# A hybrid streaming layer on one core: down projection in groups of 8, 8 and 6 blocks, later differences, row stores from GpSimd, splits queued behind their loads

## The chip, the cores and the metric

The kernel runs on one core of a Trainium2 chip. Its engines work side by side, each through a queue of its own in a fixed order: TensorE (PE in the profile, with PEld for its weight loads), VectorE (DVE), ScalarE (ACT), GpSimd (POOL) and SyncE (SP), which here only issues DMAs. The metric is the device time of one execution in microseconds (us).

## The reference

One inference step of a one-layer encoder, for 1024 rows of a new stream and 64 of a running one: a mixer (a state-space scan beside differential attention) and then a convolutional feed-forward. The change lies in the feed-forward alone:

```python
h = _rmsnorm(x, p['norm_ffn_w']) @ p['w_up']            # (1088, 1024) @ (1024, 5632)
ha, hb = jnp.split(h, 2, axis=-1)
hc, ffn_new = _causal_dwconv(ffn_past, ha, p['ffn_conv_w'], p['ffn_conv_b'])
x = x + (jax.nn.silu(hc) * hb) @ p['w_down']            # (1088, 2816) @ (2816, 1024)
```

All is float32. The kernel makes a float32 product out of three faster ones: each operand is split into a high part, which is a rounded copy, and a low part, which is the rest; the terms high x high, high x low and low x high are added up in PSUM.

## The kernel before, in words

**Strassen's scheme.** Both products of the feed-forward are done by a scheme with 7 products of half-size blocks in place of 8 (variables p = 0 to 6). The left operand is the weight, the right one the activation. Each product needs a left part and a right part, which are blocks or sums and differences of blocks. The right parts are cut in two halves of columns (s = 0, 1) of 272 tokens each.

**The way up** runs over 22 pairs f (`FT`): a pair gives 128 rows of `ha` and 128 of `hb`. A pair has 14 steps (p, s) of 12 matmuls. GpSimd multiplies the gated rows (`put`, L1242 to L1245), and the row goes to the scratch tensor `h_sc` in DRAM through SP, in two halves (L1245).

**The way down** multiplies 22 blocks of 128 rows of `h_sc`. They are taken in groups; `DOWN` lists their sizes, 6, 8 and 8. A group of size 2n has four down pairs i, so i = 0 to 3 belong to the first group, 4 to 7 to the second, 8 to 11 to the last; each of the 14 steps of a pair has 3n matmuls of 272 columns (L1390). Every result of 128 x 544 is added to the output in DRAM by a DMA that accumulates, issued by GpSimd (`send`, L1372 to L1376; the last pair of all stores its final quarter through SP, L1414). Results leave PSUM by ScalarE (p = 0 and 2) and VectorE (the other p), L1393 to L1412: these are the evacuations. Pairs 0, 3, 4, 7, 8 and 11 take all steps of s = 0 ahead of s = 1, in the order `ORD`; the others take s = 0 and 1 in turn.

**Right parts of the way down.** Three of seven are rows of `h_sc` as they are (p = 0, 2, 6); four are differences, made ahead by `differences_of` (L1304 to L1315): for a couple of rows, one of each half of a group, it loads both rows from `h_sc` into tiles `ht`, does four subtractions on VectorE and stores both to the scratch tensor `t_sc`. There are as many couples as half blocks, 11 in all. In the way up, pair f makes the couple whose later row was finished two pairs before (L1436 to L1439). The last two couples of the last group come too late for that; they are made after down pairs 1 and 2 (L1462, L1463).

`right_part` (L1320 to L1331) loads one part (n blocks x 272 columns, 408 KB or 544 KB) through SP and splits it: ScalarE makes the high part (L1042), VectorE the low one (L1043). The 14 parts of a group stay for all its four pairs. They are loaded in the last pair before the group, i.e. f = 21, i = 3 and i = 7. Each takes the place of the part that the step just done has freed (`right_parts`, L1333 to L1347). Some begin sooner: as many as there are spare places. One place is an extra one, made of two rows of the tag `fb`, in which such a part is called `ph`. Since the step order of a group isn't the order in which parts are loaded, a group can have two parts in `ph` rows.

**Buffers.** `ROWS` gives each tag a number of rows. The tag `fb` has four, for `cc` (one for each pair of the way up), `ht` (two for each couple) and `ph` (two for each part). A new tile of a tag waits until a row is free.

**Left parts** (`left_parts`, L1123 to L1165): two loads of a weight block (`w_f`, two buffers, L1129), four sums on GpSimd (L1133, L1134, L1158, L1162) and seven splits. They are made for the next pair, one or so for each step with s = 1 (`more_left`).

**What sets the order.** The instructions are written down in the order of the code, and a planner sorts them into the engines' queues by its own model of the times: where several are ready, the earlier one in the code goes first, and a later one that is ready may pass an earlier one that isn't. On the chip each queue is worked off strictly in that order, so an instruction that waits holds all that stand behind it in its queue. `tc.issue_after(x)` lets the instructions of a block stand behind x in x's queue; it is no wait for x to end.

Of the kernel before, what the change touches and what calls it, by code (L numbers as in the profile page):

```python
# [12 lines left out]
ALU = mybir.AluOpType  # L13
# [4 lines left out]
P = 128  # L18
# [11 lines left out]
FT = DFF // P  # L30
NORM = (128, 256, 192, 192, 192, 128)
LN_EXP = "natural_log_exp_and_others"
DOWN = (6, 8, 8)
ORD = (0, 1, 5, 2, 3, 4, 6)
QW = T // 4
ROWS = dict(fa=4, fb=4, fu=4, fs=2, fp=3, fh=2)
PARTS = ("b11", "t2", "b21", "t3", "t1", "t4", "b22")
# [43 lines left out]
def hybrid_layer(ctx: ExitStack, tc: tile.TileContext, xT, xt, prm, cst, rope, wvd, win, wbs, wba, wout, wup, wdn,  # L81
# [4 lines left out]
    load = nc.sync.dma_start  # L86
# [954 lines left out]
    def split(hi, lo, src):  # L1041
        S.copy(hi, src)  # L1042
        V.tensor_tensor(out=lo, in0=src, in1=hi, op=ALU.subtract)  # L1043
# [166 lines left out]
    def pair(f):  # L1210

        pre = [row("fp", "pre") for _ in range(2)]
        hb = [row("fh", "hb") for _ in range(2)]
        u1, u2 = (couple(row("fu", n)) for n in ("u1", "u2"))
        both = row("fb", "cc")
        G.memset(pre[0][:, 0:2], 0.0)
        G.tensor_copy(pre[1][:, 482:484], par[:, O_FS + 2 * f : O_FS + 2 * f + 2])
        banks = {}

        def pile(key, p, s, start):  # L1220
            if start:
                banks[key, s] = acc(QW)
            ps, w, b = banks[key, s], left[f][p], B[PARTS[p], s]
            for k in range(4):
                c = slice(P * k, P * (k + 1))
                for i, (x, y) in enumerate(((0, 0), (0, 1), (1, 0))):
                    PE.matmul(ps, w[x][:, c], b[y][:, k], start=start and k == i == 0, stop=k == 3 and i == 2,  # L1227
                              skip_group_check=not start)
            return ps

        def gate(h):

            n = 544 + 2 * h
            cc = both[:, 548 * h : 548 * h + 548]
            cw = lambda i: col(O_FW + 3 * f + i)
            act(cc[:, :n], pre[h][:, :n], AF.Identity, bias=col(O_FB + f), scale=cw(0))
            for i in range(1, 3):
                V.scalar_tensor_tensor(cc[:, :n], pre[h][:, i : i + n], cw(i), cc[:, :n], ALU.mult, ALU.add)  # L1238
            act(cc[:, :n], cc[:, :n], AF.Silu)
            return cc  # L1240

        def put(h, cc):  # L1242
            for o, d, n in ((0, 0, 544),) if h == 0 else ((0, 0, 480), (480, 482, 64)):
                G.tensor_tensor(out=hb[h][:, o : o + n], in0=hb[h][:, o : o + n], in1=cc[:, d : d + n], op=ALU.mult)  # L1244
            load(out=h_sc[P * f : P * (f + 1), 544 * h : 544 * (h + 1)], in_=hb[h][:, :544])  # L1245

        at = yield
        for _ in range(14):
            p, s = at
            qs = slice(QW * s, QW * (s + 1))  # L1250
            if p == 0:
                S.copy(u1[:, s], pile("a", p, s, True))
            elif p == 1:
                V.tensor_tensor(out=u2[:, s], in0=pile("b", p, s, True), in1=u1[:, s], op=ALU.add)
            elif p == 2:
                S.copy(pre[0][:, 2 + QW * s : 2 + QW * (s + 1)], pile("a", p, s, False))
                if s == 1:
                    G.tensor_copy(pre[1][:, 0:2], pre[0][:, 544:546])
                    cc0 = gate(0)
            elif p == 3:  # L1260
                V.tensor_tensor(out=u1[:, s], in0=pile("b", p, s, False), in1=u1[:, s], op=ALU.add)
            elif p == 4:
                V.tensor_tensor(out=hb[1][:, qs], in0=pile("c", p, s, True), in1=u1[:, s], op=ALU.add)  # L1263
            elif p == 5:
                V.tensor_tensor(out=hb[0][:, qs], in0=pile("d", p, s, True), in1=u1[:, s], op=ALU.add)
# [17 lines left out]
    def more_left(f):  # L1283
        x = next(coming, None)
        if x is not None:
            left.setdefault(f, {})[x[0]] = x[1]
# [28 lines left out]
            load(out=t_sc[P * (i + n * u) : P * (i + n * u + 1), :], in_=t[u])  # L1315

    SOURCE = {0: (h_sc, 0, 0), 1: (t_sc, 1, 1), 2: (h_sc, 1, 0), 3: (t_sc, 0, 1), 4: (t_sc, 0, 0), 5: (t_sc, 1, 0), 6: (h_sc, 1, 1)}
    parts, held, spare = {}, {}, []

    def right_part(g, p, s, at):  # L1320

        n = DOWN[g] // 2
        d, half, c = SOURCE[p]
        r = P * (first[g] + n * half)
        hi, lo = [unit(*x) if at is not None else couple(row("fb", "ph", R32), 4) for x in at or (0, 1)]
        hi, lo = hi[:, :n], lo[:, :n]
        raw = lo.bitcast(F32)
        load(out=raw, in_=d[r : r + P * n, QW * (2 * c + s) : QW * (2 * c + s + 1)].rearrange("(k p) t -> p k t", p=P))
        split(hi, lo, raw)
        parts[g, s, p] = hi, lo  # L1330
        held[s, p] = at  # L1331

    def right_parts(g, order):  # L1333

# [21 lines left out]
    def down_pair(i):  # L1356
# [22 lines left out]
        while at is not None:  # L1379
            p, s = at  # L1380
            qs = slice(QW * s, QW * (s + 1))
            key = ("a", "b", "a", "b", "c", "d", "e" if apart else "c")[p], s
            start = key not in banks
            if start:
                banks[key] = acc(QW)
            ps, w, b = banks[key], left[FT + i][p], parts[g, s, p]
            for k in range(n):
                c = slice(P * k, P * (k + 1))
                for j, (y, z) in enumerate(((0, 0), (0, 1), (1, 0))):
                    PE.matmul(ps, w[y][:, c], b[z][:, k], start=start and k == j == 0, stop=k == n - 1 and j == 2,  # L1390
                              skip_group_check=not start)
            if p == 0:
                S.copy(u1[:, qs], ps)  # L1393
            elif p == 1:
                V.tensor_tensor(out=u2[:, qs], in0=ps, in1=u1[:, qs], op=ALU.add)
            elif p == 2:
                S.copy(quadrant(2, "fp")[:, qs], ps)
                send(2, s, 0, 0)
            elif p == 3:
                V.tensor_tensor(out=u1[:, qs], in0=ps, in1=u1[:, qs], op=ALU.add)  # L1400
            elif p == 4:
                V.tensor_tensor(out=quadrant(4, "fh")[:, qs], in0=ps, in1=u1[:, qs], op=ALU.add)
                if apart:
                    V.tensor_tensor(out=u2[:, qs], in0=ps, in1=u2[:, qs], op=ALU.add)
                if end:
                    V.tensor_tensor(out=u2[:, qs], in0=base[:, qs], in1=u2[:, qs], op=ALU.add)
                send(4, s, 1, 1)
            if p == 5 and not apart or p == 3 and apart:
                V.tensor_tensor(out=quadrant(5, "fp")[:, qs], in0=banks["d", s], in1=u1[:, qs], op=ALU.add)
                send(5, s, 1, 0)  # L1410
            if p == 6:
                V.tensor_tensor(out=quadrant(6, "fh")[:, qs], in0=ps, in1=u2[:, qs], op=ALU.add)  # L1412
                if end:
                    load(out=yT[P * m : P * (m + 1), 544 + QW * s : 544 + QW * (s + 1)], in_=out[6][:, qs])  # L1414
                else:
                    send(6, s, 0, 1)
            at = yield

    for f in range(1, FT):
# [10 lines left out]
        for at, (p, s) in enumerate(steps):  # L1430
            u.send((p, s))
            if s == 1:
                more_left(f + 1)
            if f + 1 == FT:
                next(ahead_of)
            if at == 6:  # L1436
                for i, n in couples:
                    if i + n + 2 == f:
                        differences_of(i, n)  # L1439
# [7 lines left out]
    for i in range(4 * len(DOWN)):  # L1447
# [123 lines left out]
```

## Time and profile before

| | |
|---|---|
| median of 3 runs | 2449.62 us (2449.34 to 2450.59) |
| the profiled execution | 2450.28 us, of which the span from first to last instruction is 2448.5 |
| mean granted clock of TensorE | 0.998 |
| TensorE busy | 2413.0 us (99%) |
| VectorE, ScalarE, GpSimd busy | 66%, 48%, 24% |
| the way up, f = 0 to 21 | 1722 to 2200 us |
| the way down | 2193 to 2443 us |

How to read the rows that follow. A row of stages (`a:b`) has its length, then busy time and number of instructions of PE, PEld, DVE, ACT and POOL, then the granted clock, the mean busy share of the 16 DMA engines and GB/s. The number of matmuls in a stage counts those that cross its edges. A row of a timeline has start, length, engine, line, operation, tiles (out<-in) and, in brackets, how long the engine was idle before it and what ended that. A row of a group has busy time, mean ns of one, and idle time before it with what ended most of it. In a row for one line or one tile, three numbers are the shortest, the median and the longest. A row of the chain of waits has start, length and what the end of the program waited for in that time.

### The profile page before, as it was taken

How to read it: one execution, taken by the hardware profiler on the slowest of the kernel's cores; microseconds unless marked ns; L12 is line 12 of the kernel's file. 1: busy time of each engine (PE TensorE's matmuls, PEld its weight loads, DVE VectorE, ACT ScalarE, POOL GpSimd, SP SyncE). 2: the span in 40 equal slices, each digit the busy share in tenths (PEclk: the TensorE clock that was granted, in tenths of full speed). 3: DMA queues.
4: the chain of work that ended last, by engine and by line, in shares of the span. 5: the costliest groups of instructions: out<-in, count | busy, mean ns of one | idle time of the engine just before them, and what ended most of it. 6: DMA issues, size and time to landing. Idle time of an engine off the chain costs nothing. (4 is left out here: it accounts for less than half of the span.)

```text
span 2448.5 us, 44118 instructions
## 1 busy us (share of the span) xinstructions
PE 2413.0 (99%) x16824; PEld 2334.3 (95%) x16824; DVE 1606.9 (66%) x2760; ACT 1166.9 (48%) x2517; POOL 584.3 (24%) x630
## 2 busy tenths in 40 slices
PE   8999999999999999999999999999999999998999
PEld 8999999999999999998899899999999999998999
DVE  4356366755878677538677664756977777786763
ACT  7244344644666455437655453434543343353541
POOL 0000000100111001005433341013255555535533
PEclk9999999999999999999999999999999999999999
DMA  7237368443543454264797864764124234268884
GB/s 251 94 106 258 102 247 251 146 142 109 167 142 121 131 167 125 76 208 161 256 322 259 294 218 147 224 209 154 56 91 173 91 134 163 79 240 222 203 215 79
DMA packets 245670, 418.31 MB, mean 171 GB/s; under 512 B 32137, under 2 KB 168466, under 8 KB 245330
## 3 DMA queue, kind: packets, MB, share of 16 engines
q1 hardware_dynamic: 238258, 402.40, 49.6%
q0 software_dynamic: 7200, 13.09, 3.6%
q8 instruction: 132, 2.16, 0.4%
q14 instruction: 80, 0.66, 0.1%
HBM read 277.38 MB, written 138.02 MB: 170 GB/s over the span
## 5 line engine op out<-in xcount | busy, mean ns | idle before, releaser
L158 PE MATMUL mm<-xn_hi,w_hi 128*128 128x384 f32 (+1 forms) x1408 | 471.2, 335 | 1.0 <-DVE zr L550 0.9
L160 PE MATMUL mm<-xn_hi,w_lo 128*128 128x384 f32 (+1 forms) x1408 | 467.8, 332 | 0.5 <-DVE w_lo L152 0.5
L159 PE MATMUL mm<-xn_lo,w_hi 128*128 128x384 f32 (+1 forms) x1408 | 467.1, 332 | 0.0
L158 PEld LDWEIGHTS mm<-xn_hi,w_hi 128*128 128x128 f32 x1408 | 264.7, 188 | 5.9 <-DVE zr L550 1.6
L160 PEld LDWEIGHTS mm<-xn_hi,w_lo 128*128 128x128 f32 x1408 | 264.6, 188 | 3.8 <-issue 2.0
L159 PEld LDWEIGHTS mm<-xn_lo,w_hi 128*128 128x128 f32 x1408 | 264.7, 188 | 3.0 <-issue 1.6
L152 DVE TENSOR_TENSOR w_lo<-w_f,w_hi 128x1024 fp32r<-128x1024 f32 (+1 forms) x114 | 143.6, 1260 | 111.9 <-ACT w_hi L151 109.4
L151 ACT CAST w_hi<-w_f 128x1024 fp32r<-128x1024 f32 (+1 forms) x114 | 119.6, 1050 | 113.5 <-PE mx L159 52.0
L1227 PE MATMUL mx<-n,wh 128*128 128x272 f32 x1128 | 150.5, 289 | 1.9 <-ACT wh L1042 1.2
L158 PE MATMUL mm<-b_hi,w_hi 128*128 128x384 f32 (+1 forms) x448 | 151.5, 339 | 0.9 <-ACT w_hi L151 0.5
L160 PE MATMUL mm<-b_hi,w_lo 128*128 128x384 f32 (+1 forms) x448 | 148.1, 331 | 0.3 <-DVE w_lo L152 0.3
L159 PE MATMUL mm<-b_lo,w_hi 128*128 128x384 f32 (+1 forms) x448 | 147.7, 330 | 0.1
L1227 PEld LDWEIGHTS mx<-n,wh 128*128 128x128 f32 x1128 | 144.9, 188 | 2.6 <-ACT wh L1042 1.4
L1227 PE MATMUL mx<-m,w_hi 128*128 128x272 f32 x752 | 143.8, 288 | 1.3 <-DVE hb L1263 1.1
L700 ACT ACTIVATE p_t<-sc,mx 128x1024 f32<-128x1024 f32 (+5 forms) x144 | 106.3, 741 | 80.8 <-DVE mx L691 38.3
L579 DVE SCALAR_TENSOR_TENSOR cc<-pre,par,cc 128x384 f32<-128x384 f32 (+1 forms) x216 | 125.6, 584 | 15.1 <-ACT cc L577 10.9
L1043 DVE TENSOR_TENSOR wh<-w_f,wh 128x512 fp32r<-128x512 f32 (+1 forms) x100 | 93.9, 941 | 40.9 <-ACT wh L1042 40.9
L1227 PEld LDWEIGHTS mx<-m,w_hi 128*128 128x128 f32 x752 | 118.2, 188 | 2.0 <-DVE hb L1263 1.5
L1244 POOL TENSOR_TENSOR hb<-hb,cc 128x544 f32<-128x544 f32 (+2 forms) x66 | 91.0, 1393 | 108.7 <-ACT w_hi L1042 61.1
L565 POOL MEMSET pre<- 128x3 f32 x24 | 2.4, 101 | 474.8 <-DMA z_sc<-zr 378.8
L1042 ACT CAST w_hi<-ws 128x512 fp32r<-128x512 f32 (+1 forms) x68 | 41.4, 608 | 150.3 <-PE mx L1227 82.6
L1227 PE MATMUL mx<-m,w_lo 128*128 128x272 f32 x376 | 108.3, 288 | 0.0
(418 smaller groups left out, 6513.6 us busy)
## 6 DMA issues: line engine op xcount, KB each, us to landing
w_f<-in_win_dram SPq DMA_DIRECT2D x76, 512.0 KB, 3.8
w_f<-in_wup_dram SPq DMA_DIRECT2D x45, 512.0 KB, 3.5
bc<-a_sc SPq DMA_DIRECT2D x32, 512.0 KB, 5.9
h_sc<-hb SPq DMA_DIRECT2D x44, 272.0 KB, 2.1
ht<-h_sc SPq DMA_DIRECT2D x22, 544.0 KB, 4.6
t_sc<-ht SPq DMA_DIRECT2D x22, 544.0 KB, 2.9
out_dram<-yq POOLq DMA_DIRECT2D x44, 272.0 KB, 5.6
x_sc<-cc SPq DMA_DIRECT2D x48, 192.0 KB, 2.4
```

What stands on the lines that cost most here:

```text
L151: S.copy(hi, w)
L152: V.tensor_tensor(out=lo, in0=w, in1=hi, op=ALU.subtract)
L158: PE.matmul(ps, a_hi, b_hi, start=i == 0, stop=False)
L159: PE.matmul(ps, a_hi, b_lo, start=False, stop=False)
L160: PE.matmul(ps, a_lo, b_hi, start=False, stop=i == n - 1)
L565: G.memset(pre[:, 0:3], 0.0)
L579: V.scalar_tensor_tensor(cc[:, :m], pre[:, i : i + m], cw(i), cc[:, :m], ALU.mult, ALU.add)
L700: act(p_t[:n, :nk], sc[c][:n, :nk], AF.Exp, bias=mx[:n, c : c + 1], accum_out=dst)
L1042: S.copy(hi, src)
L1043: V.tensor_tensor(out=lo, in0=src, in1=hi, op=ALU.subtract)
L1227: PE.matmul(ps, w[x][:, c], b[y][:, k], start=start and k == i == 0, stop=k == 3 and i == 2, skip_group_check=not start)
L1244: G.tensor_tensor(out=hb[h][:, o : o + n], in0=hb[h][:, o : o + n], in1=cc[:, d : d + n], op=ALU.mult)
```

## The change

Five edits, all in the feed-forward:

- `DOWN` goes from (6, 8, 8) to (8, 8, 6), so that the last group is the small one; couples and weight blocks follow from it.
- The last two couples of the last group are made after i = 5 and 6 and not after i = 1 and 2. With the new groups, the last group's first couple is made in f = 21; before, its first two were made in f = 20 and 21.
- The row stores to `h_sc` are issued by GpSimd and not by SP.
- `right_part` doesn't split at once. It puts the part on a list, `landing`, and `landed(n)` splits the oldest ones until n are left. It is called at each step after the step's matmuls and evacuation, with n = 2 while parts are being loaded and with 0 at the first step after that.
- Those splits stand behind the latest evacuation of ScalarE and of VectorE (`seen`), by `issue_after`.

```diff
-DOWN = (6, 8, 8)
+DOWN = (8, 8, 6)
+LANDING = 2
...
-            load(out=h_sc[P * f : P * (f + 1), 544 * h : 544 * (h + 1)], in_=hb[h][:, :544])
+            G.dma_start(out=h_sc[P * f : P * (f + 1), 544 * h : 544 * (h + 1)], in_=hb[h][:, :544])
...
-                S.copy(u1[:, s], pile("a", p, s, True))
+                seen["ACT"] = S.copy(u1[:, s], pile("a", p, s, True))
...
-    parts, held, spare = {}, {}, []
+    parts, held, spare, landing = {}, {}, [], []
...
         load(out=raw, in_=d[r : r + P * n, QW * (2 * c + s) : QW * (2 * c + s + 1)].rearrange("(k p) t -> p k t", p=P))
-        split(hi, lo, raw)
         parts[g, s, p] = hi, lo
         held[s, p] = at
+        landing.append((hi, lo, raw))
+
+    def landed(n):
+        while len(landing) > n:
+            with tc.issue_after(seen["ACT"].ins), tc.issue_after(seen["DVE"].ins):
+                split(*landing.pop(0))
...
             if f + 1 == FT:
+                landed(LANDING)
                 next(ahead_of)
...
                 more_left(FT + i + 1)
+            if landing:
+                landed(LANDING if last else 0)
             if last:
                 next(ahead_of)
-        if i in (1, 2):
-            differences_of(*couples[len(couples) - 3 + i])
+        if i in (5, 6):
+            differences_of(*couples[i - 7])
```

The other evacuations of the way up and of the way down note themselves in `seen` in the same manner.

More of the change, by code (lines that the diff above doesn't have):

```diff
@@ L1251, in pair @@
             if p == 0:
-                S.copy(u1[:, s], pile("a", p, s, True))
+                seen["ACT"] = S.copy(u1[:, s], pile("a", p, s, True))
             elif p == 1:
-                V.tensor_tensor(out=u2[:, s], in0=pile("b", p, s, True), in1=u1[:, s], op=ALU.add)
+                seen["DVE"] = V.tensor_tensor(out=u2[:, s], in0=pile("b", p, s, True), in1=u1[:, s], op=ALU.add)
             elif p == 2:
-                S.copy(pre[0][:, 2 + QW * s : 2 + QW * (s + 1)], pile("a", p, s, False))
+                seen["ACT"] = S.copy(pre[0][:, 2 + QW * s : 2 + QW * (s + 1)], pile("a", p, s, False))
                 if s == 1:
@@ L1260, in pair @@
             elif p == 3:
-                V.tensor_tensor(out=u1[:, s], in0=pile("b", p, s, False), in1=u1[:, s], op=ALU.add)
+                seen["DVE"] = V.tensor_tensor(out=u1[:, s], in0=pile("b", p, s, False), in1=u1[:, s], op=ALU.add)
             elif p == 4:
-                V.tensor_tensor(out=hb[1][:, qs], in0=pile("c", p, s, True), in1=u1[:, s], op=ALU.add)
+                seen["DVE"] = V.tensor_tensor(out=hb[1][:, qs], in0=pile("c", p, s, True), in1=u1[:, s], op=ALU.add)
             elif p == 5:
-                V.tensor_tensor(out=hb[0][:, qs], in0=pile("d", p, s, True), in1=u1[:, s], op=ALU.add)
+                seen["DVE"] = V.tensor_tensor(out=hb[0][:, qs], in0=pile("d", p, s, True), in1=u1[:, s], op=ALU.add)
                 if s == 1:
@@ L1392, in down_pair @@
             if p == 0:
-                S.copy(u1[:, qs], ps)
+                seen["ACT"] = S.copy(u1[:, qs], ps)
             elif p == 1:
-                V.tensor_tensor(out=u2[:, qs], in0=ps, in1=u1[:, qs], op=ALU.add)
+                seen["DVE"] = V.tensor_tensor(out=u2[:, qs], in0=ps, in1=u1[:, qs], op=ALU.add)
             elif p == 2:
-                S.copy(quadrant(2, "fp")[:, qs], ps)
+                seen["ACT"] = S.copy(quadrant(2, "fp")[:, qs], ps)
                 send(2, s, 0, 0)
             elif p == 3:
-                V.tensor_tensor(out=u1[:, qs], in0=ps, in1=u1[:, qs], op=ALU.add)
+                seen["DVE"] = V.tensor_tensor(out=u1[:, qs], in0=ps, in1=u1[:, qs], op=ALU.add)
             elif p == 4:
-                V.tensor_tensor(out=quadrant(4, "fh")[:, qs], in0=ps, in1=u1[:, qs], op=ALU.add)
+                seen["DVE"] = V.tensor_tensor(out=quadrant(4, "fh")[:, qs], in0=ps, in1=u1[:, qs], op=ALU.add)
                 if apart:
@@ L1411, in down_pair @@
             if p == 6:
-                V.tensor_tensor(out=quadrant(6, "fh")[:, qs], in0=ps, in1=u2[:, qs], op=ALU.add)
+                seen["DVE"] = V.tensor_tensor(out=quadrant(6, "fh")[:, qs], in0=ps, in1=u2[:, qs], op=ALU.add)
                 if end:
```

## The prediction

> **What bounds the kernel now.** The page's head comes first, then busy time by stage, which says where TensorE loses time.
>
> ```profile
> span 2448.5 us, 44118 instructions
> PE 2413.0 (99%) x16824; PEld 2334.3 (95%) x16824; DVE 1606.9 (66%) x2760; ACT 1166.9 (48%) x2517; POOL 584.3 (24%) x630
> core 0: us, PE busy (x) PEld busy (x) DVE busy (x) ACT busy (x) POOL busy (x), PEclk, DMA share, GB/s
> 1770.40:2172.20 401.80, 401.06 (x3194) 400.37 (x3193) 297.75 (x459) 159.80 (x290) 216.11 (x233) 1.00 0.35 124
> 2172.20:2214.80 42.60, 38.13 (x298) 37.25 (x297) 38.54 (x56) 25.05 (x42) 20.99 (x19) 1.00 0.74 256
> 2214.80:2251.30 36.50, 32.67 (x254) 31.80 (x253) 24.24 (x49) 10.40 (x23) 17.79 (x19) 1.00 0.95 257
> 2251.30:2295.00 43.70, 39.69 (x296) 38.54 (x295) 33.12 (x48) 23.62 (x35) 19.73 (x16) 0.96 0.98 266
> 2295.00:2337.00 42.00, 42.00 (x337) 42.00 (x337) 23.84 (x43) 11.87 (x24) 20.77 (x19) 1.00 0.63 125
> 2337.00:2379.60 42.60, 42.59 (x340) 42.38 (x339) 32.28 (x48) 22.89 (x35) 19.00 (x16) 1.00 0.88 239
> 2379.60:2442.80 63.20, 63.17 (x504) 62.95 (x503) 27.58 (x52) 12.91 (x27) 24.45 (x25) 1.00 0.55 99
> ```
>
> TensorE is the bound, and its work doesn't change, so only its stalls can be won or made. I call the six stretches from the second row on A (last pair of the way up, f=21, and down pair i=0), B (i=1, 2), C (i=3, 4), D (i=5, 6), E (i=7, 8) and F (i=9 to 11). F runs without a stall: 504 matmuls in 63.2 us, 0.1254 us each. A pair issues 42 matmuls per unit of half a group, so 168 where the group has 8 blocks (21.1 us) and 126 where it has 6 (15.8 us). Unstalled, A would take 36.9, B 31.6, C 36.9, D and E 42.1 each. The losses are A 5.7, B 4.9, C 6.8, D 0, E 0.5, F 0: together 17.8, the 270.6 of the six less 2016 x 0.1254. The change can win little more than this: in the way up before (first row, f=2 to f=20), TensorE is busy 401 of 402 us.
>
> What ended the stalls, in the timeline of TensorE:
>
> ```profile
> 2198.11 0.52 PE L1390 MATMUL mx<-n,w_hi 128*128 128x272 f32 x2 [2.98 <-ACT w_hi L1042]
> 2240.34 1.41 PE L1390 MATMUL mm<-n,wh 128*128 128x272 f32 x9 [1.56 <-DVE u L1395]
> 2250.71 0.52 PE L1390 MATMUL mx<-m,w_hi 128*128 128x272 f32 x2 [1.54 <-DVE yq L1402]
> 2263.85 0.52 PE L1390 MATMUL mx<-m,w_hi 128*128 128x272 f32 x2 [2.32 <-ACT yq L1397]
> ```
>
> Each waits for a short evacuation or split, not for a long one: the small work stands in its engine's queue behind something that waits for a DMA. The chain of waits says which DMAs; then come SP's timeline, SP's waits from 1900 to 2200 (us in all, times, longest) and the landing times of the part loads (L1328):
>
> ```profile
> 2188.86 7.47 DMA m<-h_sc
> 2223.52 6.26 DMA t_sc<-ht
> 2229.80 7.33 DMA ht<-h_sc
> 2243.57 4.21 DMA ph<-t_sc
> 2247.87 1.11 ACT ph L1042
> 2178.39 0.36 SPq L1328 DMA_DIRECT2D n<-h_sc  x1
> 2183.45 0.33 SPq L1245 DMA_DIRECT2D h_sc<-hb  x1
> SPq L1245 <- POOL hb L1244: 202.1, 27, 10.4
> DMA to landing us min/median/max: 4.2/6.7/10.9
> ```
>
> In A, SP stands at the row store L1245 until 2183.45, because GpSimd hasn't finished the row; the part loads behind it go out late. In B the chain runs through the differences (h_sc to ht, t_sc, then ph).
>
> **The change, part by part.**
>
> *Groups 8, 8, 6.* The matmul count is the same. C becomes two pairs of 8, as E is now; E's row, with the same part loads and no differences, shows what that costs: 0.5. C's bounds are 0.2 and 3, I take 0.7, nearest to E. The cover is the 21.1 us of i=3, against 15.8 now, beside 14 loads; if the splits block as in A, the 3 is met. F becomes three pairs of 6 at 15.8 us; per pair now VectorE has 9.2 us, GpSimd 8.2, DMA share 0.55, so all fit; but weights for i=9 are asked for only in the second half of i=8. Bounds 0 and 1.5, I take 0.6.
>
> A gets larger parts, and VectorE is its tight engine:
>
> ```profile
> L1043 DVE TENSOR_TENSOR n<-n,n 128x816 fp32r<-128x816 f32 x6 | 7.3, 1238 | 1.3 <-ACT n L1042 1.3
> L1043 DVE TENSOR_TENSOR m<-m,m 128x816 fp32r<-128x816 f32 x7 | 7.0, 996 | 0.0
> L1043 DVE TENSOR_TENSOR m<-m,m 128x1088 fp32r<-128x1088 f32 x1 | 2.1, 2098 | 0.0
> L1043 DVE TENSOR_TENSOR wh<-w_f,wh 128x384 fp32r<-128x384 f32 x5 | 2.8, 568 | 0.0
> L1043 DVE TENSOR_TENSOR m<-m,m 128x1088 fp32r<-128x1088 f32 x5 | 7.2, 1440 | 4.8 <-ACT m L1042 4.8
> L1043 DVE TENSOR_TENSOR n<-n,n 128x1088 fp32r<-128x1088 f32 x5 | 6.4, 1288 | 0.0
> L1043 DVE TENSOR_TENSOR wh<-w_f,wh 128x512 fp32r<-128x512 f32 x6 | 4.5, 753 | 0.5 <-ACT wh L1042 0.5
> ```
>
> The first four rows are A's, the others E's. A part of 816 columns costs 1.10 us on average (14.3 over 13), one of 1088 1.36 (13.6 over 10): 14 x 0.26 = 3.6 more. Some 11 weight splits cost 0.19 more each: 2.0. The single 1088 split of 2.1 us is group 1's first part, which now runs two pairs early; queued behind i=3's evacuations it leaves A. VectorE goes from 38.5 to 42.0 us, while TensorE's floor goes from 36.9 to 42.1: an excess of 1.6 us becomes none.
>
> *Splits two steps behind their loads.* No instruction is added, only order: a split can't stand ahead of the evacuations of the steps up to its own. The third step after a load ends 3 x 1.5 = 4.5 us later, and the part loads land in 6.7 us at the median, so some 2 us of waiting per split can stay, where the chain now has 7.47. What could be late next is the part itself in the next pair, but that has a slack of 13 steps, near 19 us.
>
> *Row stores on GpSimd.* 44 SP issues leave, 44 GpSimd issues come.
>
> ```profile
> h_sc<-hb SPq DMA_DIRECT2D x44, 272.0 KB, 2.1
> L1375 POOL DMA_DIRECT2D out_dram<-yq x50: 843/865/1216, 2214.4 to 2442.1; - x50
> DMA to landing us min/median/max: 3.1/5.3/8.7
> ```
>
> Price: 44 x 0.865 = 38 us of GpSimd time, hidden, since it is busy 24%; in a pair of the way up it adds 1.7 to 11.4 of 21.1 (first row of the stages: 216.1 over 19 pairs). Queued behind an issue are the weight sums for the pair after, with a pair's slack. A store may land after 2.1 (as now) or 5.3 us (as GpSimd's accumulating ones); the readers come two pairs later, so either is hidden. On SP the hold before 2183.45 goes: the loads of the parts in A start up to 5.06 us earlier. With the two other parts of the change I take 2.5 for A, between 1 (E's row, doubled) and 5.7 (nothing won). A page of the Trainium skill speaks against this gain: "DMA: Bandwidth & Descriptors", Issuing engines are not separate DMA queues, says that issuing from more engines only saves the sequencer's issue time, which is small beside the transfer. The row of SP above disagrees: 202.1 us, in 27 waits, were spent at this one issue. By the page the total below would come out 2.0 later; that is the fourth rival.
>
> *Last differences after i=5, 6.* B loses its cause: no ht loads, subtractions or t_sc stores there. B's bounds are 0 (D) and 1.6 (one stall such as that of 2240.34); I take 0.2. But where do they go? A couple needs two rows of tag fb, of which there are four. In group 1 two parts live in such rows:
>
> ```profile
> 2272.73 1.65 PE L1390 MATMUL mx<-ph,wh 128*128 128x272 f32 x12
> 2274.22 0.41 PE L1390 MATMUL mx<-ph,w_hi 128*128 128x272 f32 x2
> DMA to landing us min/median/max: 3.6/4.6/7.3
> L1312 DVE TENSOR_TENSOR ht<-ht x11: 715/719/724, 1852.4 to 2238.0; 128x544 f32<-128x544 f32 x11
> DMA to landing us min/median/max: 2.6/2.9/6.3
> 2442.05 0.86 POOL L1375 DMA_DIRECT2D out_dram<-yq  x1 [0.16 <-issue]
> ```
>
> Part (1, s=0) and part (5, s=0), hi and lo each: four rows, all, in use until the second and third step of i=7. They are asked for at i=3, ahead of the couples of i=5 and 6 (now, too, ph<-t_sc took a pair of rows at 2243.57, the moment the last couple's store had landed). So the last two couples can't load before T+3.0 and T+4.5, T being i=7's start: D loses nothing, and the whole chain falls into E. The two landing rows are those of the ht loads and of the t_sc stores. The second couple: load 4.6, four subtractions 2.9, store 2.9, part load 6.7, split 1.1 on ScalarE and 1.1 on VectorE make 19.3, so part (1, s=0) stands ready at T+23.8. i=8 needs it after its first step, at T+21.1+1.1 = T+22.2. Stall: 1.6 at the medians. With the maxima (7.3, 6.3, 10.9) it is T+34.1, a stall of 11.9, and with evacuations blocked on top, as C's 6.8 now, 19; against that the planner may put later steps in between, at most some 5 steps or 5.6 us. E's floor falls to 36.9 us, and VectorE gets 5.8 more (8 subtractions) less about 5 of smaller splits: 33 of 37, as crowded as A now. Bounds for E 1 and 19; I take 6, nearer to the medians, with blocked evacuations as in B.
>
> *Tail.* The last steps become 1.1 instead of 1.5 us, so the last adds on GpSimd, 0.86 each, end nearer to the end: 0.4, bounds 0 and 0.8.
>
> **Sum.** A 2.5, B 0.2, C 0.7, D 0, E 6.0, F 0.6 make 10.0 against 17.8; with the tail 7.4 are won. The profiled execution took 2450.28 (span 2448.5, 1.8 around it), 0.66 above the median of 2449.62; taken off the median, 2442.2, faster by 0.30%. About 0.2%, 4.9 us, is what can be told from no change.
>
> **Rivals.** *First, slower.* The late differences decide: if E loses over 18.3 us (7.4 + 4.9 + 6), the kernel is slower. At E = 19 it takes 2455.2. For: all four rows held, SP a single queue in which a load of t_sc stops all behind it. Against: the medians give 1.6. Chance 0.14. *Second, the stalls only change place:* VectorE stays the bound in A (4.5), and E, as crowded as A now, loses 9: 2447.2, within 0.2%. For: 42.0 against 42.1 in A leaves no room for order. Chance 0.22. *Third, E is hidden* by reordered steps and loses 1: 2437.2. For: steps of f=21 and i=0 are already mixed. Chance 0.16. *Fourth, moving the stores does nothing*, since the hold on SP only passes to the t_sc stores behind it: A 4.5, 2444.2, at the edge of faster. Chance 0.06. The forecast has 0.42.
>
> **How the numbers follow.** Faster: 0.42 + 0.16 + half of 0.06 = 0.61; same: 0.22 + 0.03 = 0.25; slower 0.14. The range, 2435 to 2453, takes in the third rival and an E of 16.8, and leaves out most of the first and the corner where A, C and E all reach their low ends. The forecast's own range is 2438 to 2445.
>
> **What would show it.** Right: SP's waits at L1245 are gone and GpSimd has 94 DMA issues; two clean 8-block pairs where C is; B's stretch without ht; ht loads first at i=7's second step, and TensorE's longest stall at the start of i=8, ended by a split or evacuation behind a DMA from t_sc. Wrong: ht loads during i=5 or 6 (the rows were free), a stall in f=21 ended by a split that waits for its load, or stalls in F ended by weights.

## Result and the profile after

The changed kernel takes 2459.76 us (median of 6 executions, 2454.65 to 2467.72), the kernel before, on the same chip, 2450.11 (2446.74 to 2452.68). The ratio is 1.0045, with a 95% interval from 1.0025 to 1.0066: it is slower by some 0.45%, where 0.3% faster was predicted. The profiled execution is the shortest of the six, 2454.65, but not because of its feed-forward: its first matmul of f=0 starts at 1717.3 us, 5.1 earlier than in the kernel before, in a part of the program that the change doesn't touch. From there to the end it takes 735.6 us and the kernel before 726.1. This difference, 9.5, is the one to explain; it is close to that of the medians, 9.65. (The other five executions weren't profiled.)

The page's head of the changed kernel, and the stages (f=2 to 20 first, then A to F as in the prediction, divided at this kernel's pairs; columns as before):

```profile
span 2452.9 us, 44090 instructions
PE 2409.5 (98%) x16824; PEld 2333.3 (95%) x16824; DVE 1608.9 (66%) x2760; ACT 1164.7 (47%) x2517; POOL 600.1 (24%) x674
...
1765.20:2169.00 403.80, 400.50 (x3194) 400.29 (x3193) 295.69 (x457) 156.97 (x289) 229.86 (x273) 1.00 0.37 124
2169.00:2216.90 47.90, 44.54 (x338) 43.56 (x337) 42.05 (x55) 28.91 (x42) 23.03 (x20) 0.96 0.82 275
2216.90:2259.60 42.70, 42.45 (x339) 42.22 (x338) 22.96 (x44) 11.10 (x23) 22.48 (x22) 1.00 0.67 147
2259.60:2301.80 42.20, 42.20 (x339) 42.20 (x338) 39.05 (x50) 25.02 (x36) 21.47 (x15) 1.00 0.87 235
2301.80:2343.90 42.10, 42.10 (x338) 42.10 (x337) 20.49 (x38) 11.04 (x23) 19.16 (x18) 1.00 0.61 125
2343.90:2396.10 52.20, 41.29 (x297) 39.91 (x296) 33.16 (x55) 20.96 (x36) 16.25 (x14) 0.87 0.82 249
2396.10:2443.70 47.60, 47.60 (x380) 47.38 (x378) 25.01 (x55) 11.46 (x27) 21.16 (x24) 1.00 0.67 117
```

With 168 matmuls a pair (126 in the last group) at 0.1254 us the floors are 42.1 for A to D, 36.9 for E and 47.4 for F. B, C, D and F have next to no stalls left. A loses 5.8 and E 15.3. (The expectations below say 15.4, from the first start to the last end.) The sum of the prediction, term by term:

| us lost | before | forecast | after | after, less forecast |
|---|---|---|---|---|
| A: f=21, i=0 | 5.7 | 2.5 | 5.8 | +3.3 |
| B: i=1, 2 | 4.9 | 0.2 | 0.6 | +0.4 |
| C: i=3, 4 | 6.8 | 0.7 | 0.1 | -0.6 |
| E: i=7, 8 | 0.5 | 6.0 | 15.3 | +9.3 |
| F: i=9 to 11 | 0 | 0.6 | 0.2 | -0.4 |
| after TensorE's last matmul | 5.7 | 6.1 | 9.2 | +3.1 |
| f=1 to 20 | 1.6 | 1.6 (hidden) | 3.5 | +1.9 |

The last column adds up to 17.0, which leads from 7.4 won to 9.6 lost. Now the places. First E: TensorE's stalls in it, in the timeline, then two rows of the timeline of ScalarE, then that of SP, then three pieces of the chain of waits:

```profile
2367.85 0.52 PE L1396 MATMUL mm<-n,w_hi 128*128 128x272 f32 x2 [1.50 <-ACT w_hi L1043]
2380.63 2.78 PE L1396 MATMUL mm<-n,wh 128*128 128x272 f32 x9 [8.00 <-ACT wh L1043]
...
2387.61 0.66 PE L1396 MATMUL mx<-n,w_hi 128*128 128x272 f32 x2
2388.07 0.43 PE L1396 MATMUL mx<-n,w_lo 128*128 128x272 f32 x1
```

```profile
2380.07 0.51 ACT L1043 CAST wh<-w_f 128x384 fp32r<-128x384 f32 x1 [0.18 <-DMA w_f<-in_wdn_dram]
2383.40 0.87 ACT L1043 CAST m<-m 128x816 fp32r<-128x816 f32 x1 [2.82 <-DMA m<-t_sc]
```

```profile
2347.04 2.31 SPq L1309 DMA_DIRECT2D ht<-h_sc  x4
2354.22 0.32 SPq L1316 DMA_DIRECT2D t_sc<-ht  x1
2357.52 1.30 SPq L1316 DMA_DIRECT2D t_sc<-ht  x2
2361.98 0.33 SPq L1316 DMA_DIRECT2D t_sc<-ht  x1
2363.11 0.36 SPq L1329 DMA_DIRECT2D ph<-t_sc  x1
2366.69 6.87 SPq L1130 DMA_DIRECT2D w_f<-in_wdn_dram  x2
2376.71 2.58 SPq L1329 DMA_DIRECT2D m<-t_sc  x1
```

```profile
2366.69 6.13 SPq L1130
...
2373.61 9.77 DMA m<-t_sc
...
2383.40 0.88 ACT m L1043
```

The four `ht` loads go out from 2347.04 on, 3.1 us after i=7 began at 2343.9: there the rows come free, as forecast. The first load from `t_sc` can go 16 us later, at 2363.11, when i=8 is 2 us away. From there to 2376.71 eight such parts, one from `h_sc` and two weight blocks are asked for, and SP stands 6.87 us in issuing the two weight loads. These two are for i=9: a pair has seven weight splits, and the seven of i=8 are done by 2367.8. The planner has put the first step of i=9 ahead of the rest of i=8 in TensorE's queue. That step needs the first of the two blocks, which lands only at 2379.99, 13.30 us after its issue; ScalarE splits it at once (2380.07, after 0.18 of waiting for the load), and here TensorE's 8.00 us end. The step of i=8 behind it needs a part from `t_sc` whose load could go only after the weight loads, at 2373.61, and which lands 9.77 us later; this gives the stalls of 0.92 and 0.49, and the chain of waits runs through it. So TensorE would have stood still for most of this time for either of the two; this is argued from the one trace, as no run cures one of them alone.

Of E's 15.3 us, 10.9 are stalls (8.00, 1.50, 0.92 and 0.49). Another 3.2 are matmuls that start further apart at a lower granted clock (0.87 in the stage): 21 of them 0.23 apart instead of 0.1254 (the row of 2387.61, two matmuls in 0.46), and four, right after the stalls, some 0.4. The rest is the modelled ends of the matmuls ahead of the stalls.

The Trainium skill, "TensorE: Matmul & The Clock Gate", What's actually happening, has TensorE at half rate after an idle window of about 3.4 us until it has been busy for such a window. The stall of 8.00 us agrees: 0.23 apart behind it, and 0.13 again from 2389.2 on, 3.8 us after the last stall. Other stalls here don't: one of 3.29 us in f=3 (below) isn't followed by a lower clock, but shorter ones are. A has a granted clock of 0.96 with a longest stall of 1.89 us, and so has C of the kernel before, with 2.32. So in this case the length of a stall alone doesn't tell whether the clock falls.

In f=3, a stall that the kernel before hasn't, and the landing time of the row stores:

```profile
1789.86 0.52 PE L1228 MATMUL mx<-m,w_hi 128*128 128x272 f32 x2 [3.29 <-DVE hb L1264]
...
h_sc<-hb POOLq DMA_DIRECT2D x44, 272.0 KB, 4.4
```

At the end, the last pieces of the chain of waits, which in the kernel before ended with TensorE and one VectorE evacuation:

```profile
2441.77 0.85 POOL out_dram L1381
2442.62 0.80 issue
2443.44 0.84 POOL out_dram L1381
2444.28 0.88 POOLq L1576
```

### The profile page after: what moved, and what is told of

The parts are those of the page before. It is cut to its first block, busy times and chain, and to the rows that moved or that the text cites. A ratio compares the mean times of both kernels' runs of the same rounds, so it can differ in the third digit from the quotient of the medians.

```text
span 2452.9 us, 44090 instructions
## 1 busy us (share of the span) xinstructions
PE 2409.5 (98%) x16824; PEld 2333.3 (95%) x16824; DVE 1608.9 (66%) x2760; ACT 1164.7 (47%) x2517; POOL 600.1 (24%) x674
## 5 line engine op out<-in xcount | busy, mean ns | idle before, releaser
L580 DVE SCALAR_TENSOR_TENSOR cc<-pre,par,cc 128x384 f32<-128x384 f32 (+1 forms) x216 | 125.3, 583 | 15.0 <-ACT cc L578 10.9
L1245 POOL TENSOR_TENSOR hb<-hb,cc 128x64 f32<-128x64 f32 (+2 forms) x66 | 91.5, 1401 | 95.9 <-DVE hb L1266 53.3
L568 POOL COPY pre<-pre 128x3 f32<-128x3 f32 x48 | 14.8, 309 | 373.7 <-ACT pre L569 166.7
```

What stands on the lines that cost most here:

```text
L568: G.tensor_copy(pre[:, 0:3], tail)
L580: V.scalar_tensor_tensor(cc[:, :m], pre[:, i : i + m], cw(i), cc[:, :m], ALU.mult, ALU.add)
```

## The experiments

Each kernel was timed against the kernel before on the same chip, whose median lay between 2453.5 and 2454.0 in these comparisons. The table puts all of them side by side: losses in us by stage in one profiled execution (from first matmul to the next stage's first matmul, less 0.1254 for each matmul; D is 0 but for 2.1 in e10 and 0.4 in e16), the time from TensorE's last matmul to the end of the span, and the ratio of the times with its interval. One execution's stages vary by some us, and the row of the kernel before was taken where its median was 2449.6; the ratios decide.

| kernel | f=1 to 20 | A | B | C | E | F | end | ratio to before |
|---|---|---|---|---|---|---|---|---|
| before | 1.6 | 5.6 | 4.9 | 6.9 | 0.3 | 0.1 | 5.7 | 1 |
| changed | 3.5 | 5.8 | 0.5 | 0.1 | 15.3 | 0.2 | 9.2 | 1.0045 [1.0025, 1.0066] |
| e1: changed, differences early | 3.6 | 7.0 | 3.4 | 0.6 | 0.0 | 4.0 | 9.2 | 0.9999 [0.9990, 1.0008] |
| e3: before, differences late | 2.7 | 6.1 | 0.0 | 7.6 | 20.4 | 0.1 | 5.9 | 1.0059 [1.0046, 1.0073] |
| e4: before, groups 8, 8, 6 | 8.7 | 3.2 | 3.5 | 5.0 | 0.0 | 0.2 | 7.5 | 0.9982 [0.9973, 0.9991] |
| e5: before, stores on GpSimd | 3.1 | 8.2 | 6.8 | 7.2 | 1.0 | 0.1 | 7.6 | 1.0022 [1.0014, 1.0031] |
| e6: before, splits queued | 2.4 | 5.2 | 4.9 | 7.2 | 0.1 | 0.1 | 5.8 | 0.9993 [0.9982, 1.0003] |
| e7: changed, stores on SP | 7.1 | 5.8 | 2.7 | 0.4 | 16.2 | 0.2 | 7.4 | 1.0042 [1.0030, 1.0055] |
| e8: e1, stores on SP | 9.3 | 5.8 | 5.5 | 1.3 | 0.0 | 2.1 | 7.5 | 1.0003 [0.9993, 1.0012] |
| e10: changed, one `ph` part | 4.6 | 6.0 | 0.1 | 2.9 | 0.0 | 5.5 | 9.3 | 1.0015 [1.0006, 1.0024] |
| e14: changed, one couple late | 4.5 | 5.8 | 3.5 | 0.6 | 6.2 | 1.5 | 9.2 | 1.0014 [1.0002, 1.0025] |
| e12: e4, nine pairs' stores on GpSimd | 0.8 | 6.3 | 9.3 | 1.2 | 0.0 | 0.2 | 8.3 | 0.9985 [0.9975, 0.9996] |
| e15: e12, splits of group 1 queued | 0.8 | 4.8 | 5.2 | 1.1 | 0.1 | 0.3 | 8.2 | 0.9960 [0.9948, 0.9971] |
| e16: e15, f=21's subtractions on GpSimd | 0.9 | 7.3 | 3.0 | 1.1 | 0.2 | 0.2 | 8.0 | 0.9972 [0.9961, 0.9983] |

**The late differences taken back (e1), and alone (e3).** In e1, on the changed kernel; e3 makes the same edit the other way on the kernel before.

```diff
-        if i in (5, 6):
-            differences_of(*couples[i - 7])
+        if i in (1, 2):
+            differences_of(*couples[len(couples) - 3 + i])
```

> The changed kernel with the last two couples' differences put back after i=1 and i=2; the other three parts stay. Theory (late differences): the loss at the start of group 2 comes from the chain load, subtractions, store, part load, split that can't begin before i=7's third step, so here the stretch i=7, i=8 keeps under 2 us of stalls instead of 15.4, i=1 and i=2 get back at most 1 to 5 us, and the median is 2444 to 2449, below the kernel before or level with it. Rival (small last group): the loss comes from refilling fourteen parts under two 6-block pairs, with 36.9 us instead of 42.1; then the stretch i=7, i=8 still loses over 8 us with this order and the median stays at 2455 or above.

> The kernel before, groups of 6, 8, 8, with nothing changed but the last two couples' differences, which run after i=5 and i=6. Theory (late differences): the rows are held here as well, so the stretch i=7, i=8 rises from 0.5 us of stalls to 10 or more, i=1 and i=2 win at most 4.9, and the median is 5 to 10 us above the kernel before. Rival (small last group): with an 8-block last group the chain has 5 us more and is hidden, the gain at i=1 and i=2 is left, and the median is 2 to 5 us below the kernel before.

E of e1, and E of e3, where it has two pairs of 8 blocks (floor 42.1):

```profile
2354.00:2390.90 36.90, 36.90 (x296) 36.90 (x295) 30.23 (x48) 20.68 (x36) 14.96 (x15) 1.00 0.84 213
```

```profile
2333.30:2395.80 62.50, 48.46 (x338) 46.55 (x337) 39.20 (x54) 24.35 (x35) 17.30 (x14) 0.86 0.82 250
```

E's loss goes to zero with the groups and the queued splits as they are, and comes (20.4) without them, in a last group of 8. So it is due to the late differences; the small last group isn't needed for it, and the rival falls. E of e3 has the same picture, a stall of 7.78 us that ends at a weight split. B wins what was forecast in e3 (0.0 for 4.9). The median of e3 is 14.3 above the kernel before, more than the 5 to 10 expected, since E lost more than was thought. The price by the ratios: 0.59% alone, and 1.0045 less 0.9999, 0.46% or 11 us, within the change. The median of e1 missed its expectation, though: 2453.89, level with the kernel before and not below, so something else in the change costs what the groups win (see e8).

**The parts alone: groups (e4), stores (e5), splits (e6).** Each is one part of the change, made on the kernel before as the diff in the section on the change has it.

> The kernel before with nothing changed but the groups of the down projection, 8, 8, 6. Theory (late differences): the change of groups by itself wins at i=3, i=4, now two 8-block pairs, some 3 to 6 us, and loses at most 3 at i=7, i=8: the median is between 1 and 5 us below the kernel before. Rival (small last group): the loss moves to i=7, i=8 and is as large as 8 us or more there, so the median is 3 to 8 us above the kernel before.

> The kernel before with nothing changed but the 44 row stores of the way up, issued by GpSimd. Theory: SP's waits at this store (202.1 us in 27) go, the loads of the parts in f=21, i=0 start up to 5 us sooner and that stretch loses 2 to 3 instead of 5.7 us: the median is 1 to 4 us below the kernel before, and the time after TensorE's end stays at 5.7 us. Rival (a cost elsewhere): the stretch keeps over 4.5 us of stalls, and the time after TensorE's end rises to about 9 us as in the changed kernel, since GpSimd's closing drain grows with the transfers that it has issued: the median is then 2 to 4 us above the kernel before.

> The kernel before with nothing changed but the parts' splits, queued two steps behind their loads. Theory (the stores spoil f=21, i=0): queueing takes the blocked evacuations out of i=3, i=4 (6.8 us of stalls before, under 2 here) and does no harm in f=21, i=0 (5.7 before, 5 or less here); the median is 3 to 7 us below the kernel before. Rival (the queue itself spoils f=21, i=0): the splits come later there, that stretch loses 7 or more, what i=3, i=4 win is given back, and the median is within 2 us of the kernel before.

The groups alone are faster by 0.18%, 4.4 us (median 2449.39), as expected; but C wins less than the expected 3 to 6 (5.0 for 6.9), and the stages of this execution don't show where the rest is won. The stores alone cost 0.22%, 5.4 us (2458.95), in the rival's direction and somewhat more; the end rose to 7.6 and not to 9. The splits alone, 2451.37, can't be told from no change, and C isn't cured by them (7.2): that theory fell. The four ratios alone add up to 1.0056, against 1.0045 for all together, whose interval holds this.

What the stores cost is seen in two places of e5. VectorE's waits in f=3 (1785 to 1815):

```profile
DVE hb L1263 <- DMA h_sc<-hb: 4.1, 1, 4.1
DVE hb L1265 <- DMA h_sc<-hb: 1.7, 1, 1.7
```

An evacuation into `hb` waits for a store of the old `hb` row to land, since tag `fh` has two rows; TensorE then waits 2.85. The other place is the end. By the column "end" the rows fall in clear steps: 5.7 to 5.9 with 50 GpSimd DMAs and groups 6, 8, 8; 7.4 to 7.5 with 50 and 8, 8, 6; 7.6 with 94 and 6, 8, 8; 9.2 to 9.3 with 94 and 8, 8, 6. So 44 more DMAs cost 1.8 or 1.9, though they were all issued in the way up, and the small last pairs cost 1.6 to 1.8, since the last results go out later after TensorE's end: the last one lands 4.8 us after it in e4 and 3.2 in the kernel before.

**The stores back on SP, in the changed kernel (e7) and with the differences early (e8).** `G.dma_start` in `put` becomes `load` again.

> The changed kernel with nothing taken back but the row stores of the way up, which go back to SP. Theory (terms add): the GpSimd stores cost the same here as alone in the kernel before, so this is 4 to 6 us faster than the changed kernel: no stall in f=3 (3.3 in the changed kernel), 7.4 us after TensorE's end instead of 9.2, and i=7, i=8 still lose 12 or more; the median is level with the kernel before or up to 5 us above it. Rival (the stores matter for i=8, since SP's queue and the landing of transfers differ): i=7, i=8 lose under 8 us and the median is below the kernel before.

> The changed kernel without two of its parts: row stores of the way up back on SP, the last differences back after i=1 and i=2; groups of 8, 8, 6 and the queued splits stay. Theory (the GpSimd stores cost about 5 us: a stall of 3 in f=3, 1.8 in the closing drain): against the same kernel with GpSimd stores, which was level with the kernel before, this is 4 to 7 us faster, so 4 to 7 us below the kernel before; no stall in f=3, and 7.4 us from TensorE's end to the span's end instead of 9.2. Rival (the queued splits cost it): the median is within 2 us of the kernel before, as with the GpSimd stores.

Neither theory held, and e8 is where its rival had it, within 2 us of the kernel before: the end is shorter by 1.8, as expected, and the stall in f=3 is gone, but the ratios are those with GpSimd stores (1.0042 for 1.0045, 1.0003 for 0.9999), and E still loses 16.2 in e7. E8 is e4 with the queued splits and nothing else, so the pair also prices these with groups of 8, 8, 6: 1.0003 for 0.9982, intervals that don't overlap, so queueing all splits costs some 0.2%, 5 us, and takes back what the groups win. In one execution each, C wins 3.7 by it (1.3 for 5.0), and A, B and F lose 6.5.

With groups of 8, 8, 6 and stores on SP the way up stalls elsewhere, 7.1 to 9.3 us. E4 shows it as well; first its timeline of TensorE in f=17, then its chain of waits there:

```profile
2109.80 0.52 PE L1227 MATMUL mm<-m,w_hi 128*128 128x272 f32 x2 [2.92 <-DVE hb L1263]
```

```profile
2101.15 2.36 POOL hb L1244 x2
2103.51 0.02 issue
2103.52 0.32 SPq L1245
2103.84 0.05 issue
2103.89 4.08 DMA ht<-h_sc
...
2109.40 0.36 DVE hb L1263
```

The row store waits for GpSimd's product and holds the `ht` load behind it in SP's queue; VectorE's subtraction is late and holds the evacuation. That is the hold that the prediction saw in A, but in a pair in which a couple is differenced. Why it bites with 8, 8, 6 and hardly with 6, 8, 8 (1.6 to 2.7 in before, e3 and e6) stays open.

**Only the stores that hold something (e12).** On e4:

```diff
+            put_to = nc.gpsimd.dma_start if f in (5, 6, 7, 8, 13, 14, 15, 16, 20) else load
-            load(out=h_sc[P * f : P * (f + 1), 544 * h : 544 * (h + 1)], in_=hb[h][:, :544])
+            put_to(out=h_sc[P * f : P * (f + 1), 544 * h : 544 * (h + 1)], in_=hb[h][:, :544])
```

> The kernel before with groups of 8, 8, 6 and with the row stores of nine pairs only (those ahead of a pair in which differences are taken) issued by GpSimd, 18 stores instead of 44. Theory (two effects of the stores): on SP a store holds the ht load behind it, which costs 4 to 7 us in pairs 7 to 9, 16, 17 with these groups; on GpSimd a store lands later and costs 3 us in pair 3. So here both are gone, f=1 to 20 lose under 2.5 us (8.2 with the groups alone), the time after TensorE's end grows by the share of transfers that GpSimd issues, to 8.1 us (7.5 at 50 issues, 9.2 at 94), and the median is 3 to 7 us below that with the groups alone, so 7 to 11 below the kernel before. Rival (the stalls in the way up are chance, not the store): f=1 to 20 lose over 5 us in spite of it and the median is within 2 us of the groups alone, 4 below the kernel before.

Both effects are as the theory has them: f=1 to 20 lose 0.8 for 8.7, and the end takes 8.3 us with 68 GpSimd DMAs, between 7.5 and 9.2. The median isn't: 2449.46, and by the ratios (0.9985 for 0.9982) e12 is level with the groups alone. In this execution, what the way up won came back in A and B (15.6 for 6.7).

**The held rows (e10, e14).** E10 drops the second `spare.append(None)`, so one part less lives in rows of `fb`; e14 makes one couple after i=1 and the last after i=6.

> The changed kernel with one spare place fewer for the parts of groups 1 and 2, so that one part instead of two lives in rows of tag fb, and two of the four rows are free for the late differences. Theory (held rows): the first ht loads go out at the end of i=5, some 24 us before i=7's third step, where they go in the changed kernel; both couples' chains end before i=8, the stretch i=7, i=8 loses under 4 us instead of 15.4, and the median is 8 to 12 us below the changed kernel, so about level with the kernel before, less what one place fewer costs at i=3, i=4 (0 to 4). Rival (whatever the rows, the chain after i=5 is too late or too crowded): the ht loads leave at i=5's end and the stretch i=7, i=8 still loses 10 us or more.

> The changed kernel with one of its two late couples back after i=1; only the last one is differenced after i=6. Theory (latency of one chain): a part needs both couples' rows, so what counts is the last couple's load, subtractions, store, part load and split; the first load still can't leave before rows of tag fb come free, at i=7's second step, and the stretch i=7, i=8 loses 9 us or more of the 15.4. Rival (crowding: eight loads and stores and eight subtractions at once): half of them are gone and the stretch loses under 6 us. The median follows: 3 to 6 below the changed kernel by the theory, 8 to 12 by the rival.

The couples' DMAs in e10, and E of e10:

```profile
L1309 SPq DMA_DIRECT2D ht<-h_sc x4: 320/388/657, 2270.8 to 2299.4; - x4
L1316 SPq DMA_DIRECT2D t_sc<-ht x4: 320/330/1822, 2282.5 to 2316.6; - x4
```

```profile
2344.10:2381.00 36.90, 36.90 (x296) 36.90 (x295) 28.47 (x47) 20.57 (x37) 14.11 (x14) 1.00 0.89 218
```

With two rows free, the loads leave from 2270.8 on, in i=3 and i=4, even before the i=5 expected, and E loses nothing: the held rows are what makes the late differences cost. One place less costs elsewhere (C 2.9, D 2.1, F 5.5), and the kernel takes 2455.09, 0.15% slower than before; by the ratios that is 7 us below the changed kernel, a bit less than the 8 to 12 expected. With one late couple of two (e14) E loses 6.2 of 15.3, just above the rival's bound of 6, and the theory's 9 fails: crowding counts for more than the length of one chain, whose loads still go out 3.1 us after i=7's start. The median, 2457.12, is by the ratios 7.6 us below the changed kernel (1.0014 for 1.0045), between the two expectations.

**Queueing where it helps (e15), and A's bound (e16).** E15 is e12 with the change's `landing` for the parts of group 1 alone; e16 has the subtractions of the couple of f=21 on GpSimd besides.

```diff
-        landing.append((hi, lo, raw))
+        if g == 1:
+            landing.append((hi, lo, raw))
+        else:
+            split(hi, lo, raw)
```

> As the kernel with groups of 8, 8, 6 and nine pairs' stores on GpSimd, and with the splits queued for the parts of group 1 alone; those of group 0 and group 2 are issued with their loads. Theory (queueing helps where evacuations stand behind splits, i=3, i=4, and hurts in f=21, i=0): f=21, i=0 lose about 3 us as with the groups alone, not 5.8, and i=3, i=4 under 2 instead of 4.9; the median is 2 to 5 us below that of the same kernel without queueing. Rival (what queueing wins at i=3, i=4 depends on the later start that it gives to group 0): i=3, i=4 lose 4 or more and the median is that of the same kernel without queueing, within 2 us.

> As the kernel with groups of 8, 8, 6, nine pairs' stores on GpSimd and splits queued for group 1 alone, and the four subtractions of the couple that is differenced in f=21 go to GpSimd, which leaves VectorE 2.9 us less work in f=21, i=0; GpSimd's take about 1.35 us each, 2.5 longer in all for that chain. Theory (VectorE's work bounds f=21, i=0: about 42 busy in a floor of 42.1, whatever the order of stores and splits): the stretch loses 2 to 3 us instead of 4.8 and the median is 1 to 3 below that kernel, 11 to 13 below the kernel before. Rival (the arrival of parts bounds it): the stretch loses 4.5 or more, the median is the same or above.

E15 is the fastest of all, 2443.66 (2441.20 to 2447.10): 0.40% faster than the kernel before and so faster than both kernels. It beats e12 by 5.8 us, the expected direction and a bit more; but its stages win that in A and B and not in C, where e12 already lost only 1.2; and A keeps 4.8 where 3 was expected. So that queueing for group 1 helps is shown, and by which way is not. A of e15, and A of e16:

```profile
2168.90:2215.80 46.90, 43.20 (x338) 42.33 (x337) 40.09 (x54) 28.19 (x41) 24.80 (x21) 1.00 0.79 268
```

```profile
2168.50:2217.90 49.40, 45.32 (x339) 44.88 (x338) 41.63 (x54) 28.13 (x41) 30.57 (x24) 0.93 0.79 271
```

E16's A loses 7.3 for 4.8, as the rival has it, and the median is 2445.59. But VectorE's busy time in A didn't fall (41.6 for 40.1): other work took the place of the subtractions. So taking these away doesn't help, and whether VectorE bounds A isn't settled.

## Why the prediction was wrong

**E, the step that failed.** "The second couple: load 4.6, four subtractions 2.9, store 2.9, part load 6.7, split" found the place, the cause (four held rows, loads from T+3.0 on) and the direction of this term, but its size was that of one part at median times: 6, where 15.3 was measured. The prices of the couples' transfers are medians over the whole program, and most couples are made in the way up, where the DMA share is 0.35. Here the landing times of the part loads in E were, in us, from shortest to longest

```profile
DMA to landing us min/median/max: 5.7/10.2/13.2
```

instead of 6.7 at the median. The sum has the late part landed at T+21.6; the part that TensorE waited for last landed at 2383.38, T+39.4. It had to wait for SP to issue the two weight loads for i=9, whose first block was late as well. The sum had no weights in E at all; it had them late in F, with 0.6. Nor had it the 3.2 us of slower matmuls. What it left out besides is the time of the DMA engines. Two stretches of E, with the DMA share and GB/s at the end:

```profile
2343.90:2363.10 19.20, 19.20 (x155) 19.20 (x154) 13.23 (x23) 6.00 (x12) 6.19 (x5) 1.00 0.98 311
2363.10:2387.00 23.90, 12.99 (x80) 11.61 (x79) 14.00 (x22) 12.91 (x22) 9.44 (x10) 0.76 1.00 294
```

An estimate from these rows: two couples are eight transfers of 544 KB, some 14 us at 311 GB/s, on top of the 31 us that the DMA engines are busy in E of e1 (0.84 of 36.9). That makes 45 us of transfers for a floor of 36.9, so some 8 us would be lost even with the queues in the best order. No run takes this apart from the order in SP's and TensorE's queues; e14, with half of these transfers, lost 6.2. The upper bound of 19 held; the value inside was taken too near the medians.

**A, 5.8 for 2.5.** The step was "On SP the hold before 2183.45 goes: the loads of the parts in A start up to 5.06 us earlier". SP no longer waits at the row store, and the first part loads did start sooner, 1.6 us after f=21's start (2170.6, for 2.6 before). But the hold itself only passed on. SP's longest wait on GpSimd in A of the changed kernel:

```profile
SPq L1309 <- POOL hb L1245: 4.6, 1, 4.6
```

A load of `ht` now waits for GpSimd's product, and the part loads behind it go out from 2181.24 on, 12.2 us after f=21's start; before, they went from 2184.35 on, 12.2 us after it as well. The fourth rival had such a passing on, though to the `t_sc` stores. Then the loads took longer to issue and to land. The part loads of A before, then after:

```profile
L1328 SPq DMA_DIRECT2D m<-t_sc x4: 360/446/1187, 2176.8 to 2193.5; - x4
...
DMA to landing us min/median/max: 4.6/6.6/8.0
```

```profile
L1329 SPq DMA_DIRECT2D m<-t_sc x4: 360/1247/1608, 2173.6 to 2190.6; - x4
...
DMA to landing us min/median/max: 3.7/8.2/10.0
```

The parts are of 544 KB for 408, and the DMA share is 0.82 for 0.74; that this is why they land later is argued, not shown. VectorE's busy time came out as forecast, 42.05 for 42.0. In one execution each, A loses 3.2 with the groups alone (e4), 8.2 with the stores alone (e5) and 5.8 with groups and queued splits (e8), so neither the stores nor the queued splits are seen to help A. The second rival had A nearly right (4.5), for a reason, VectorE's load, that e16 couldn't confirm.

**Stores.** "The readers come two pairs later, so either is hidden" looked at the readers of `h_sc` alone. Who waited was the next writer of the `hb` row: 3.3 us in f=3. And the GpSimd time of the issues was hidden as forecast (44 at 0.57 us, 25 us for the 38 of the price), but not the 1.8 at the end. The rule that the prediction set against this part (the Trainium skill, "DMA: Bandwidth & Descriptors", Issuing engines are not separate DMA queues) gives nothing won by moving all 44 stores, and the changed kernel agrees (1.0045 with them, 1.0042 without); on the kernel before they even cost 0.22%. The runs disagree with its reason, since the hold in SP's queue costs more than the time of an issue (f=1 to 20 lose 8.7 us in e4 and 0.8 in e12, in one execution each).

**Queued splits.** The sum took them as a gain in A and C without a cost. They do cure C once the groups are changed, but as a whole they cost 0.2% there (e8 beside e4), and they pay only for the parts of group 1 (e15 beside e12).

**Tail, 3.5 for 0.4:** the half that comes of the small last pairs was named and sized too small, the half of the GpSimd DMAs wasn't seen.

**Right:** B, C, D and F within 0.7 each; SP's waits at the store gone (others took their place); the `ht` loads at i=7's third step; the groups alone faster; TensorE's longest stall in i=8, though at a weight split and not at an evacuation or split behind a part. For C the credit was misplaced: neither groups (5.0) nor queued splits (7.2) cure it alone, both together do (e1 0.6, e8 1.3), and so do the groups with other stores (e12 1.2). The first rival had the mechanism; it decided at an E of 15.3 and not 18.3, because A, the end and the way up fell short as well.

## What to carry to other kernels

Work that is put off meets what is already due at its new place: add up the time of all transfers that are asked for in the same stretch, weights included, against the length of the stretch, and take the landing times of the busiest stage that the trace has, not medians. When a store moves to another queue, look at who writes its source buffer next, not only at who reads its target. A hold in a queue is worth taking away just where something urgent stands behind it, and where it doesn't pass to the next instruction in the queue. Moving 18 of 44 stores took away the loss in the way up, though the median followed only when splits were queued as well, and the fastest kernel here keeps three parts of the change in that narrower form and leaves out the late differences.

## What the runs showed of the hardware

- The time from TensorE's last matmul to the end grew with the number of DMAs that GpSimd had issued in the whole program, though most had landed long before: 5.7, and 7.6 with 44 more; 7.5, 8.0 to 8.3 and 9.2 with 50, 68 and 94 in the other groups. Some 0.04 us each; why wasn't tried.
- A DMA issue on SP, 0.3 us as a rule, stood for several us when transfers backed up: 6.87 us for two weight loads in E (6.13 of it for the first), and 1.25 at the median for part loads from `t_sc` into `m` in A.
